# Smaller first loads in order of use, other buffers for GLA factors and gates, and new slot counts in a one-core hybrid decoder step

## The chip, the cores and the metric

One core of one Trainium2 chip runs the whole kernel. The metric is the device time of one execution in microseconds; three runs of the kernel before gave 998.02, 1000.86 and 1001.59 us, median 1000.86. One further execution was profiled: 999.49 us, of which 997.7 us lie between its first and its last instruction (the span).

## The reference, cut to what matters

One step of a two-layer recurrent trunk with 2048 features, over 256 prompt tokens and 8 x 8 sample tokens, 320 columns in all:

```
layer 0: proj = rmsnorm(x) @ w_in                     # q, k, v, gates, low-rank decay inputs
         q_a, k_a, v_a = silu(conv4(proj[qkv]))       # 8 heads x 128
         o_a, S_a = gated_delta_rule(q_a, k_a, v_a, g, beta, S_a)
         gk = log_sigmoid(proj[lr] @ w_lr + b) / 16   # "decays"
         o_b, S_b = gla(q_b, k_b, v_b, gk, S_b)       # 4 heads x (128, 256)
         x += concat(o_a, o_b) * silu(gate) @ w_out
layer 1: x += (rg_lru(conv4(rmsnorm(x) @ w_x)) * silu(rmsnorm(x) @ w_g)) @ w_out
out:     rmsnorm(x), and all recurrent and convolution states of prompt and samples
```

## The kernel before, in words

Features lie on the 128 partitions and the 320 token columns along the free axis. Every dense product is run as 30 groups of 512 output features. A group (`run_group`, L246) holds four PSUM accumulators of 128 x 320 and goes through 8 chunks `kc`; a chunk is 2 x 128 input features (index `a`) times 512 outputs, 512 KB of weights `wst`. `split_chunk` (L231) splits each half chunk into a rounded part `wh` (ScalarE) and a remainder `wl` (VectorE), `split_x` (L1403) does the same for the activations (`xh`, `xl`), and `product` (L255) issues three matmuls of 320 columns for each pair of 128 x 128 (wh xh, wh xl, wl xh; L261). A chunk is thus 24 matmuls and a group 192.

All other work lies between these matmuls. It is written as generators in three queues: `hi`, `lo` and `tails`. After each product pair half `slot` (L130) advances the front of each queue by one step, so a group gives 64 steps. The table `WAITS` says how many empty steps a generator leaves at each named place (`wait`, L66). `until(flag)` (L412) advances `lo` without matmuls between until a flag is set; `drain` empties a queue. The framework orders the instructions of each engine by this order and by its own estimates of readiness; each engine then runs its own list in order. SyncE (SP) issues nearly all loads.

The groups in order: 0 Q, 1 K, 2 V, 3 V second half, 4 K second half, 5 Q second half of the delta rule (`evac_conv_a`, L417); 6 to 9 the GLA's q, k, v, v (`evac_plain`); 10 to 13 the four gates (`evac_gate`, L1366); 14 to 17 the output product; 18 to 25 the LRU inputs and gates; 26 to 29 the last product. On the queue `lo` stand, one after another: `small_work`, `gla_decays` (L1174), `delta_half(0)`, `delta_half(1)`, `delta_sample` (L878), `gla` (L1321). Their places in this order, in steps after group 0 began: the first two start after group 1 (step 128), `gla` is appended after group 8. After group 13 all queues are drained. `sample_states(0, 16)` runs in groups 14 to 17 and `sample_states(16, 24)` (L982) in groups 26 to 29; the latter loads the samples' GLA states, updates and stores them.

`gla_decays` keeps its factors in two tiles that take both buffers of the tag VP, which the V halves of groups 2 and 3 need; so group 2 calls `until("gd")` in its last chunk. Gates 0 and 1 keep their sample columns in the tiles `SMPQ` and `SMPK` that `delta_sample` reads, so they call `until("gdns")` in the last chunk of group 10. At the end y is scaled in pieces (L1916 to L1919) and each piece is stored when it is ready.

Of the kernel before, what the change touches and what calls it, by code (L numbers as in the profile page):

```python
# [71 lines left out]
def hybrid_step(ctx, tc, x_cols, w_dense, w_small, w_lr, w_gate, par_a, par_b, par_c, gains, head_rows,  # L72
# [141 lines left out]
    def load_first():  # L214

        t = wst[0] = wpool.tile([P, 2, 512], F32, name="wst", tag="wst", bufs=3)
        for n in (0, 256):
            sp.dma_start(t[:, 0, n:n + 256], w_dense[0, 0, :, 0, n:n + 256])
        load_x(sp, 1, 1)
        sp.dma_start(t[:, 1], w_dense[0, 0, :, 1])  # L220
# [25 lines left out]
    def run_group(g, hook=None, n_lo=1):  # L246
# [3 lines left out]
        for kc in range(8):  # L250
# [18 lines left out]
            for f in range(4):  # L269
                if hook:  # L270
                    hook(kc, f)
                for a in range(2):
                    if i or a:
                        product(f, a)
                    if a == 0:
                        slot(n_lo)
# [140 lines left out]
    def evac_conv_a(slot_name, half, part):  # L417
# [8 lines left out]
        def late():  # L426
            if part == 2:
                until("gd")
            p_ = env["keep"] if part == 0 else env["lay0b"]
            st["t"] = p_.tile([P, 4, TP], F32, name="qkv", tag=("QP", "KP", "VP")[part], bufs=2)  # L430
            env[slot_name, half] = st["t"]
# [742 lines left out]
    def gla_decays():  # L1174
# [3 lines left out]
        r3 = [env["lay0b"].tile([P, 4, TP], dt, name="lr3", tag="VP", bufs=2).rearrange("p a b -> p (a b)")[:80]  # L1178
              for dt in (F32, F32R)]
# [186 lines left out]
    def evac_gate(idx, dst):  # L1366
        st = {}

        def late():
# [6 lines left out]
            until("gdns")  # L1376
            if idx == 3:
                until(("gp", 1))
            p_ = env["keep"] if tag == "QP" else env["lay0b"]
            st["z"] = (p_.tile([P, 4, TP], F32, name="zp", tag=tag, bufs=2), env["SMP" + tag[0]].rearrange("p u q e x -> p (u q e x)")[:, :4 * TS].rearrange(  # L1380
                             "p (f t) -> p f t", f=4))
# [318 lines left out]
    load_chunk(1)  # L1700
    load_x(sp, 2, 2)
    load_x(sp, 4, 2)
    load_chunk(2)
# [85 lines left out]
    with tc.issue_after(env["xs"][0].ins):  # L1789
        x_tile(1)  # L1790
        split_chunk(0, 1)
    with tc.issue_after(env["xs"][1].ins):
        for a in range(2):
            split_chunk(1, a)
    hi.append(start_work())

    def hook0(kc, f):
        if f == 0 and kc < 4:
            load_x(sp, 8 + 2 * kc, 2)
        if f % 2 and kc < 7:  # L1800
            k = 2 * (kc + 1) + f // 2
            x_tile(k)
# [19 lines left out]
    for nm in ("qs16", "kns", "krs"):  # L1822
        env[nm] = lay0b.tile([P, 4, TS], F32, name=nm)

# [91 lines left out]
    for m, f, n in ((0, 0, 1), (0, 1, 1), (0, 2, 2), (1, 0, 4), (2, 0, 4), (3, 2, 2)):  # L1916
        t = ob[m][:, f:f + n]
        dve.tensor_mul(t, t, row[:, None, :].to_broadcast([P, n, NT]))  # L1918
        sp.dma_start(y_cols[m, :, f:f + n], t)  # L1919
# [62 lines left out]
```

## Time and profile before

| what | value |
|---|---|
| three runs | 998.02, 1000.86, 1001.59 us |
| profiled execution, whole | 999.49 us |
| its span | 997.7 us |
| TensorE matmul busy | 971.5 us |
| VectorE, ScalarE, GpSimd busy | 708.4, 525.5, 229.9 us |
| mean granted TensorE clock | 0.992 |

TensorE is the engine that is nearly always busy. Where it stands, and where its clock is at the lower level, is read from its list of waits, from the timeline and from windows of time; the granted clock is 1.00 at 2.4 GHz and 0.50 at 1.2 GHz.

### The profile page before, as it was taken

Reading aid. Unit: us, or ns where it says so; the run is one execution under the profiler, and the core shown is the slowest. Engines: PE = TensorE matmul, PEld = TensorE weight load, DVE = VectorE, ACT = ScalarE, POOL = GpSimd, SP = SyncE. Lnnn points to the kernel's source line nnn. Section 1 sums busy time; section 2 is a strip of 40 time slices with the busy share of each in tenths; the row PEclk is TensorE's granted clock in tenths of the full one; section 3 lists DMA queues with packets and bytes.
Section 4 is the critical chain, followed back from the end, with each engine's and each line's share of the span. In section 5 each row is a group of like instructions: output and inputs, shape, how many; then the busy total and the mean of one; then the engine's idle time right before and its main releaser. Section 6 shows DMA issues by size and latency. Waiting matters only on the chain. (4 is left out here: it accounts for less than half of the span.)

```text
span 997.7 us, 18739 instructions
## 1 busy us (share of the span) xinstructions
PE 971.5 (97%) x6917; PEld 952.5 (95%) x6917; DVE 708.4 (71%) x1483; ACT 525.5 (53%) x1077; POOL 229.9 (23%) x365
## 2 busy tenths in 40 slices
PE   8999999999999999999999999999999999999995
PEld 8989999999999998899999999999999999999995
DVE  6789877675454556687677789867969668776753
ACT  7567674456333444665233344547685885333441
POOL 4520026702083020152112333200010000054000
PEclk8999999999999999999999999999999999999998
DMA  8535435534455266243766887654546435568742
GB/s 290 168 122 144 135 111 175 144 117 127 139 154 163 87 227 223 70 136 108 270 224 199 256 264 243 217 158 145 158 123 191 131 125 170 166 184 309 265 139 105
DMA packets 63927, 171.62 MB, mean 172 GB/s; under 512 B 16248, under 2 KB 21388, under 8 KB 63324
## 3 DMA queue, kind: packets, MB, share of 16 engines
q1 hardware_dynamic: 58852, 160.35, 51.3%
q0 software_dynamic: 2720, 8.66, 2.4%
q10 hardware_dynamic: 2264, 1.42, 0.4%
q8 instruction: 54, 0.88, 0.4%
q14 instruction: 37, 0.30, 0.1%
HBM read 155.73 MB, written 14.68 MB: 171 GB/s over the span
## 5 line engine op out<-in xcount | busy, mean ns | idle before, releaser
L261 PE MATMUL acc<-xh,wh 128*128 128x320 f32 x1920 | 600.6, 313 | 5.9 <-ACT wh L236 2.4
L261 PE MATMUL acc<-xh,wl 128*128 128x320 f32 x1920 | 595.3, 311 | 2.3 <-DVE wl L237 2.3
L261 PE MATMUL acc<-xl,wh 128*128 128x320 f32 x1920 | 596.8, 311 | 0.0
L236 ACT ACTIVATE wh<-wst 128x512 fp32r<-128x512 f32 x479 | 278.4, 623 | 326.7 <-PE acc L261 237.8
L237 DVE TENSOR_TENSOR wl<-wst,wh 128x512 fp32r<-128x512 f32 x479 | 337.2, 736 | 144.4 <-ACT wh L236 137.8
L261 PEld LDWEIGHTS acc<-xh,wh 128*128 128x128 f32 x1920 | 361.9, 189 | 9.4 <-ACT wh L236 5.4
L261 PEld LDWEIGHTS acc<-xh,wl 128*128 128x128 f32 x1920 | 362.0, 189 | 3.2 <-DVE wl L237 2.9
L261 PEld LDWEIGHTS acc<-xl,wh 128*128 128x128 f32 x1920 | 362.4, 189 | 1.3
L458 DVE SCALAR_TENSOR_TENSOR yc<-slab,pa,yc 128x344 f32<-128x344 f32 x72 | 42.2, 605 | 2.7 <-ACT yc L101 2.3
L1572 POOL MEMSET aa<- 128x32 f32 x4 | 0.7, 164 | 117.7 <-ACT rr L1559 66.7
L693 POOL TENSOR_TENSOR xi<-xi,tmp 128x60 f32<-128x60 f32 (+24 forms) x62 | 26.6, 429 | 4.9
L691 POOL TENSOR_TENSOR tmp<-ab,xi 128x60 f32<-128x60 f32 (+24 forms) x62 | 25.6, 412 | 4.8
L1002 POOL TENSOR_TENSOR uvkh<-uvk,uvkh 32x256 fp32r<-32x256 f32 (+1 forms) x8 | 12.3, 1542 | 56.8 <-DMA ugt<-in_state_gla_dram 51.4
L1007 POOL TENSOR_TENSOR uvm<-uvh,rm 96x512 fp32r<-96x512 f32 x16 | 20.5, 1307 | 0.3
L1114 POOL DMA_DIRECT2D out_s_delta_dram<-ust x8 | 6.0, 751 | 62.3 <-DVE ust L1111 62.3
L748 POOL TENSOR_TENSOR so<-so,mhalf 128x4 f32<-128x4 f32 x4 | 4.4, 1103 | 67.3 <-DVE so L747 67.3
L1111 DVE SCALAR_TENSOR_TENSOR ust<-ust,es,sn 128x128 f32<-128x128 f32 x64 | 17.8, 340 | 3.0 <-PE sn L1107 3.0
L462 ACT ACTIVATE qkv<-yc 128x256 f32<-128x256 f32 x24 | 10.0, 415 | 16.1 <-DVE yc L458 16.1
L1503 DVE SCALAR_TENSOR_TENSOR yc<-slab,pb,yc 128x344 f32<-128x344 f32 x32 | 17.6, 573 | 0.7 <-ACT yc L1501 0.6
L101 ACT ACTIVATE yc<-slab,pa 128x344 f32<-128x344 f32 x24 | 13.3, 576 | 8.6 <-DVE slab L350 7.0
L349 DVE TENSOR_TENSOR slab<-acc,rb 128x256 f32<-128x256 f32 x36 | 14.9, 417 | 2.6 <-PE acc L261 2.4
L376 POOL MEMSET slab<- 128x12 f32 x10 | 1.2, 124 | 65.5 <-DVE xc L1510 36.3
(464 smaller groups left out, 1019.0 us busy)
## 6 DMA issues: line engine op xcount, KB each, us to landing
wst<-in_w_dense_dram SPq DMA_DIRECT2D x239, 512.0 KB
st<-in_state_delta_dram SPq DMA_DIRECT2D x8, 512.0 KB
st<-in_state_gla_dram SPq DMA_DIRECT2D x4, 1024.0 KB
ust<-in_state_delta_dram SPq DMA_DIRECT2D x8, 512.0 KB
out_s_delta_dram<-ust POOLq DMA_DIRECT2D x8, 512.0 KB, 4.7
ugt<-in_state_gla_dram SPq DMA_DIRECT2D x8, 512.0 KB
out_s_gla_dram<-ugt POOLq DMA_DIRECT2D x8, 512.0 KB, 7.1
x0r<-in_x_cols_dram SPq DMA_DIRECT2D x8, 320.0 KB
```

The lines of the kernel that those rows point to most:

```text
L101: return act.activation(out, in_, AF.Identity, scale=scale)
L236: act.activation(h, wst[i][:, a, :], AF.Copy)
L237: env["last_split"] = dve.tensor_sub(l, wst[i][:, a, :], h.bitcast(F32))
L261: mm = pe.matmul(o, (h, h, l)[j][:, fs], (xh, xl, xh)[j][k], start=(k == 0 and j == 0), stop=(k == KT - 1 and j == 2))
L349: dve.tensor_mul(xp[:, 3:259], xp[:, 3:259] if acc is None else acc[:, :256], rb[:, :256])
L458: dve.scalar_tensor_tensor(y[:, :n], xp[:, j:j + n], pa[:, ft, j:j + 1], y[:, :n], op0=OP.mult, op1=OP.add)
L691: behind(pool.tensor_mul(tv, ab[:, j, j + 1:, None].to_broadcast([P, m, w]), xi[:, j:j + 1, :w].to_broadcast([P, m, w])))
L693: behind(pool.tensor_add(xi[:, j + 1:, :w], xi[:, j + 1:, :w], tv))
L1002: pool.tensor_sub(o, t[rows, :, cols], o.bitcast(F32))
L1007: pool.tensor_mul(m, src.bitcast(F32)[:, None, :].to_broadcast([R, 4, P]), rm4[:R, :, None].to_broadcast([R, 4, P]))
L1111: dve.scalar_tensor_tensor(s_, s_, es[:, col:col + 1], ps[:, b, :], op0=OP.mult, op1=OP.add)
L1503: dve.scalar_tensor_tensor(y[:, :n], xp[:, j:j + n], pb[:, ft, 2 + j:3 + j], y[:, :n], op0=OP.mult, op1=OP.add)
```

## The change

It does the following.

- Start: the first three weight chunks are loaded as half chunks and the activations x in single tiles, in the order x0, w0a (still in two quarters), x1, w0b, x2, w1a, x3, w1b, x4, w2a, x5, w2b (a and b are the halves `a` = 0 and 1). Activation tiles 1 to 3 and the half chunks up to w1b are split before the first group begins. In chunks 1 and 2 the products go through all four accumulators for `a` = 0 first, then for `a` = 1.
- The two tiles of the GLA factors move from the tag VP to one buffer of QP and one of KP. `until("gd")` moves from the V groups (2, 3) to the second halves of K and Q (groups 4, 5).
- Gates 0 and 1 get sample tiles of their own (`zs0`, `zs1`); only gate 3 still calls `until("gdns")`.
- The y stores of rows 1 and 2 are cut in two.
- Some 50 entries of `WAITS` change. Those that the prediction uses are in the table below; sums of steps are for the whole generator.

| generator | entries changed | steps before | after |
|---|---|---|---|
| small_work | .2 0 to 1, .3 0 to 6 | 3 | 10 |
| gla_decays | .1 13 to 16, .3 4 to 7, .4 9 to 10 | 70 | 86 |
| delta_half, each | quad_a.1 3 to 2, invert32.3 3 to 2, quad_out.3 3 to 0, quad_b.1 22 to 23, .2 1 to 4, .5 0 to 2, .9 2 to 1 | 218 | 214 |
| delta_sample | invert.2 6 to 2, .1 12 to 8, .4 9 to 8, .5 14 to 8, .7 11 to 10, .8 0 to 1, quad_a.1 | 159 | 112 |
| gla | gla.1 2 to 0, .2 4 to 5, .3 3 to 2, .4 19 to 20, gla_out.1 6 to 3, .2 2 to 3 | 214 | 196 |
| sample_states(16, 24), a pair of units | .8 12 to 2, .10 6 to 10 | 36 | 42 |

The diff without the table of waits:

```diff
     def load_first():
-        t = wst[0] = wpool.tile([P, 2, 512], F32, name="wst", tag="wst", bufs=3)
-        for n in (0, 256):
-            sp.dma_start(t[:, 0, n:n + 256], w_dense[0, 0, :, 0, n:n + 256])
-        load_x(sp, 1, 1)
-        sp.dma_start(t[:, 1], w_dense[0, 0, :, 1])
+        for i in range(3):
+            t = wst[i] = wpool.tile([P, 2, 512], F32, name="wst", tag="wst", bufs=3)
+            for a in range(2):
+                if i or a:
+                    load_x(sp, 2 * i + a, 1)
+                w = 512 if i or a else 256
+                for n in range(0, 512, w):
+                    sp.dma_start(t[:, a, n:n + w], w_dense[0, i, :, a, n:n + w])
...
-                    if i or a:
+                    if 0 < i < 3:
+                        product((2 * f + a) % 4, f // 2)
+                    elif i or a:
                         product(f, a)
...
         def late():
-            if part == 2:
+            if part < 2 and half:
                 until("gd")
...
-        r3 = [env["lay0b"].tile([P, 4, TP], dt, name="lr3", tag="VP", bufs=2).rearrange("p a b -> p (a b)")[:80]
-              for dt in (F32, F32R)]
+        r3 = [t.rearrange("p a b -> p (a b)")[:80] for t in env["lr3"]]
...
             tag = ("QP", "KP", "", "VP")[idx]
-            until("gdns")
             if idx == 3:
+                until("gdns")
                 until(("gp", 1))
...
-            st["z"] = (p_.tile([P, 4, TP], F32, name="zp", tag=tag, bufs=2), env["SMP" + tag[0]].rearrange("p u q e x -> p (u q e x)")[:, :4 * TS].rearrange(
-                             "p (f t) -> p f t", f=4))
+            zs = env["zs"][idx] if idx < 2 else env["SMPV"].rearrange("p u q e x -> p (u q e x)")[:, :4 * TS].rearrange(
+                "p (f t) -> p f t", f=4)
+            st["z"] = (p_.tile([P, 4, TP], F32, name="zp", tag=tag, bufs=2), zs)
...
     load_first()
-    load_chunk(1)
-    load_x(sp, 2, 2)
-    load_x(sp, 4, 2)
-    load_chunk(2)
     load_x(sp, 6, 2)
...
-    with tc.issue_after(env["xs"][0].ins):
-        x_tile(1)
-        split_chunk(0, 1)
-    with tc.issue_after(env["xs"][1].ins):
-        for a in range(2):
-            split_chunk(1, a)
+    for k in range(1, 4):
+        with tc.issue_after(env["xs"][k - 1].ins):
+            x_tile(k)
+            split_chunk(k // 2, k % 2)
...
-        if f % 2 and kc < 7:
+        if f % 2 and 0 < kc < 7:
...
+    env["lr3"] = [p_.tile([P, 4, TP], dt, name="lr3", tag=tag, bufs=2)
+                  for p_, tag, dt in ((ws0, "QP", F32), (lay0b, "KP", F32R))]
+    env["zs"] = [ws0.tile([P, 4, TS], F32, name=f"zs{i}") for i in range(2)]
...
-    for m, f, n in ((0, 0, 1), (0, 1, 1), (0, 2, 2), (1, 0, 4), (2, 0, 4), (3, 2, 2)):
+    for m, f, n in ((0, 0, 1), (0, 1, 1), (0, 2, 2), (1, 0, 2), (1, 2, 2), (2, 0, 2), (2, 2, 2), (3, 2, 2)):
```

## Rows read from the trace of the kernel before

**Rows 1.** The page: busy time and share of the span of each engine.

```profile
PE 971.5 (97%) x6917; PEld 952.5 (95%) x6917; DVE 708.4 (71%) x1483; ACT 525.5 (53%) x1077; POOL 229.9 (23%) x365
```

**Rows 2.** The chain of work that ended last, a stretch of it with nothing between the matmuls: start, duration, what and how many.

```profile
637.00 51.91 PE acc L261 x354
```

**Rows 3.** The list of waits for TensorE over the whole span: who waited for whom, us in total, times, longest.

```profile
PE ot L964 <- DVE on L959: 3.0, 2, 1.6
PE acc L261 <- ACT wh L236: 2.4, 2, 1.5
PE acc L261 <- DVE wl L237: 2.3, 2, 1.8
PE acc L261 <- ACT xh L101: 1.7, 1, 1.7
...
PE got L1168 <- DVE gon L1164: 1.2, 2, 0.6
PE acc L261 <- DVE slab L350: 1.2, 1, 1.2
...
PE smt L498 <- DVE sm L487: 0.9, 1, 0.9
...
PE cum L528 <- DVE gt L521: 0.4, 1, 0.4
```

**Rows 4.** Windows at the start: stretch and its length, busy us (and instructions) of PE, PEld, DVE, ACT and POOL, then granted clock, DMA share and GB/s.

```profile
0.00:7.00 7.00, 5.58 (x27) 4.96 (x27) 3.08 (x10) 3.66 (x6) 5.24 (x13) 1.00 0.67 192
7.00:8.00 1.00, 1.00 (x7) 1.00 (x8) 0.66 (x1) 0.00 (x0) 0.00 (x0) 1.00 0.88 305
8.00:9.00 1.00, 1.00 (x7) 0.75 (x6) 0.00 (x0) 0.00 (x0) 0.00 (x0) 1.00 1.02 399
9.00:10.75 1.75, 0.02 (x2) 0.01 (x1) 1.00 (x2) 1.66 (x4) 0.00 (x0) 1.00 1.01 405
...
10.75:12.40 1.65, 1.65 (x10) 1.65 (x10) 1.65 (x5) 0.85 (x2) 0.36 (x1) 0.73 1.01 410
...
12.40:18.20 5.80, 5.80 (x23) 5.80 (x23) 4.80 (x12) 5.55 (x13) 3.28 (x7) 0.50 0.80 278
```

**Rows 5.** The timeline at the start: start, duration, engine, line, operation, out<-in, count, and in brackets the idle time before and what ended it.

```profile
6.31 0.63 ACT L236 ACTIVATE wh<-wst 128x512 fp32r<-128x512 f32 x1 [0.59 <-DMA wst<-in_w_dense_dram]
6.97 0.69 DVE L237 TENSOR_TENSOR wl<-wst,wh 128x512 fp32r<-128x512 f32 x1 [0.67 <-ACT wh L236]
...
9.09 1.15 ACT L236 ACTIVATE wh<-wst 128x512 fp32r<-128x512 f32 x2 [2.15 <-DMA wst<-in_w_dense_dram]
...
10.14 1.46 ACT L101 ACTIVATE xh<-ob,gcol 128x320 fp32r<-128x320 f32 x3
10.74 0.58 PEld L261 LDWEIGHTS acc<-xh,wh 128*128 128x128 f32 x4 [1.99 <-ACT xh L101]
```

**Rows 6.** Windows around the end of group 2, the same columns as rows 4.

```profile
105.00:110.90 5.90, 5.90 (x41) 5.72 (x39) 5.59 (x14) 5.06 (x10) 0.00 (x0) 1.00 0.04 11
110.90:112.90 2.00, 0.17 (x3) 0.01 (x1) 2.00 (x5) 0.60 (x1) 0.00 (x0) 1.00 0.00 0
...
113.90:117.30 3.40, 3.40 (x15) 3.40 (x15) 3.40 (x8) 1.14 (x3) 0.00 (x0) 0.50 0.69 190
```

**Rows 7.** The timeline of VectorE there (L1207 is the scan of the decays), and TensorE's next matmul.

```profile
110.95 0.81 DVE L1207 TENSOR_TENSOR_SCAN gk<-seg,gk 128x320 f32<-128x320 f32 x1
...
112.89 0.57 PE L261 MATMUL acc<-xh,wl 128*128 128x320 f32 x2 [1.83 <-DVE wl L237]
```

**Rows 8.** The timeline of TensorE: the first instruction of `delta_half(0)`, `delta_half(1)` and `delta_sample`, and the output transposes of `delta_sample`.

```profile
122.75 0.60 PE L580 MATMUL kt<-ident,qkv 128*128 128x128 f32 x4
...
239.82 0.60 PE L580 MATMUL kt<-ident,qkv 128*128 128x128 f32 x4
...
357.24 0.60 PE L580 MATMUL kt<-ident,smpK 128*128 128x128 f32 x4
...
397.78 0.33 PE L964 MATMUL ot<-ident,on 128*128 128x128 f32 x1 [1.42 <-DVE on L959]
...
410.05 0.30 PE L964 MATMUL ot<-ident,on 128*128 128x128 f32 x1 [1.61 <-DVE on L959]
```

**Rows 9.** The timeline at the end of `gla`: the issues of its sample states on SP, its two state products, the first matmul of group 14, and the last transposes.

```profile
479.88 1.18 SPq L1332 DMA_DIRECT2D st<-in_state_gla_dram x2
...
491.17 1.93 PE L1357 MATMUL gpo<-st,gqm 128*32 128x256 f32 x32
...
493.13 0.81 SPq L1332 DMA_DIRECT2D st<-in_state_gla_dram  x2
...
503.23 1.93 PE L1357 MATMUL gpo<-st,gqm 128*32 128x256 f32 x32
...
505.44 0.49 PE L261 MATMUL acc<-xh,wh 128*128 128x320 f32 x1
...
507.86 0.44 PE L1168 MATMUL got<-ident,gon 128*128 128x128 f32 x2 [0.61 <-DVE gon L1164]
```

**Rows 10.** The chain of waits in groups 26 and 27.

```profile
913.92 9.73 DMA wst<-in_w_dense_dram
```

**Rows 11.** Windows at the end, the same columns as rows 4 (y is being stored).

```profile
989.00:990.00 1.00, 0.00 (x0) 0.00 (x0) 1.00 (x2) 0.00 (x0) 1.00 (x1) 1.00 0.88 311
990.00:991.00 1.00, 0.00 (x0) 0.00 (x0) 1.00 (x2) 0.00 (x0) 0.45 (x1) 1.00 0.85 329
991.00:992.00 1.00, 0.00 (x0) 0.00 (x0) 1.00 (x1) 0.00 (x0) 0.00 (x0) 0.57 0.72 279
```

40 rows, old and new, of the table WAITS are left out of this document.

## The prediction

> **What bounds the kernel now.** I read the page's busy times first: the matmul engine is busy 97% of the span, every other engine 71% or less [rows 1]. Then the chain of waits for a stretch without interruptions: 354 matmuls in 51.91 us, 146.6 ns each [rows 2]. The program has 30 x 192 = 5760 such matmuls, 845 us at that pace. The change touches no matmul's size or number, so all it can win is time in which TensorE stands, time in which its clock is low, and the tail after the last matmul. Third, therefore, TensorE's own list of waits [rows 3]: the rows shown add up to 13.1 us. Fourth, the windows around the two longest, for the granted clock: 0.50 (1.2 GHz) from 12.4 to 18.2 us, after TensorE stood from 9.0 to 10.75 [rows 4], and from 113.9 to 117.3, after it stood from 110.9 to 112.9 [rows 6]. Elsewhere I found no stretch at the low level before the last matmul. Each gap thus cost its own length and something after it.
>
> **The start.** Chunk 1 was one load of 512 KB; ScalarE waited for it until 9.09, split both halves (1.15 us for two) and only then turned to x2 at 10.14; TensorE went on at 10.74 after an idle of 1.7 us [rows 3, 5]. The new order asks for less before that point: x0, w0a, x1, w0b, x2, w1a are 3 x 164 KB + 3 x 262 KB = 1.28 MB (in thousands of bytes), where before x2 stood behind all of chunk 1. The old run moved 7.0 x 192 = 1.34 MB by 7.0 us [rows 4], so w1a should land near 6.8. ScalarE ends w0b's split at 6.94; then x2 (a third of 1.46 = 0.49 us) and w1a's split (0.58) take it to 8.0, and VectorE's remainder of 0.69 to 8.7 [rows 5]. TensorE is busy with chunk 0 until 9.0, so the gap closes with 0.3 us to spare. x3 and w1b (1.70 MB) come by 8.1 at the 305 to 399 GB/s of the next rows [rows 4]; their splits end near 9.9, and the four products of `a` = 0 (12 x 0.147 = 1.76 us) keep TensorE until 10.8. Behind the added issues on SP stand x6/x7 and chunk 3; chunk 3 waits for chunk 0's buffer in any case, so I cost them at nothing; without that cover it would be some 0.4 us an issue. Gain: 1.7 us of idle. The clock: 5.8 us at 0.50 and 1.65 us at 0.73 [rows 4] are worth 0.5 x 5.8 + 0.27 x 1.65 = 3.3 us; I take 3.1, since some tiny matmuls of the masks fall into it. Sum 4.8, with 0 and 5.1 as ends.
>
> What speaks against it is the speed of small loads. The Trainium skill, "DMA: Bandwidth & Descriptors", section "Rules for kernel authors", asks for 1 MiB and more in a DMA and for the merging of small ones. Rows 4 agree in kind: 305 GB/s at 7 to 8 us, with pieces still in the queues, against 399 to 405 when only large ones ran. By its row for 64 KB (138 GB/s) an estimate is 1.28 MB / 138 = 9.3 us, and the gap would stay.
>
> **The decays.** `until("gd")` in group 2's last chunk forced the rest of `gla_decays` into the same few microseconds as the group's evacuation. In steps: 128 + 3 + 70 = 201 was its natural end, and the call comes at 128 + 57 = 185. VectorE ran the scans (0.81 us each) ahead of the split that TensorE needed, and TensorE stood for 1.83 us [rows 7]; the DMA share fell to 0.04 and 0.00 because no weight buffer came free [rows 6]. After: 128 + 10 + 86 = 224, no V group calls, and the call in group 4 comes at 256 + 57 = 313, long after. `delta_half(0)` stands behind it on `lo`: it is appended only after group 2's conv tails (four of 9 empty steps), and its first transposes ran at 122.75 [rows 8], which I count as step 222; 2 steps later is nothing. Gain 1.8 idle and half of 3.4 us of clock = 1.7: 3.5, ends 1.0 and 4.0. The wait of `cum` (0.4) gets 6 steps of cover: 0.4 [rows 3].
>
> **The samples of the delta rule.** The three first transposes lie 117.1 and 117.4 us apart [rows 8], and the table of waits gives 218 steps for a `delta_half`: 0.54 us a step, so the count can be trusted. `delta_sample` had 159 steps, 86 us, yet its second output transposes ran at 410.05, only 53 us after its first instruction: `until("gdns")` squeezed it, and TensorE stood 1.42 and 1.61 us at these transposes. After, nothing squeezes it before group 13, and it has 112 steps, 10 of them between the scaling and the transposes. Gain 3.0, ends 1.5 and 3.0. Where this goes: it starts 6 steps earlier (8 fewer in the halves, 2 more before) and ends 112 x 0.54 - 3 = 57 us after 357.24, at about 414 on the old clock, 4 us later than before. `gla` follows with 196 steps, 106 us: 520, where it ended at 508 before [rows 9]. Group 14 began at 505.4 [rows 9]. It needs the last sample GLA outputs for its last quarter, 144 matmuls or 21 us in; 15 us late plus the gating and split of about 3 us still fits, with 3 us to spare. I cost it at 1 us, because TensorE already stood 0.6 us twice at `got` [rows 3] and the space there shrinks from 8 to 6 steps; ends 0 and 8.
>
> **Last group's states.** In groups 26 and 27 TensorE waited 2.4 us for `wh` [rows 3], behind a weight load that took 9.73 us [rows 10] while state loads and stores came in pairs. The units are now evenly spaced (22 and 20 steps instead of 24 and 12), but the first fetches keep their places. Half of it: 1.2, ends 0 and 2.4. `sample_states(0, 16)` and the LRU entries move work where TensorE hardly stands; cost 0.5, ends -0.5 and 2.
>
> **The tail.** From 989 to 992 the DMA share was 0.88, 0.85 and 0.72 [rows 11]; 0.55 us of transfer were missed while VectorE scaled whole rows. Halves start the stores earlier: 0.4, ends -0.2 and 0.55.
>
> **The sum** against the profiled execution of 999.49 us: 4.8 + 3.5 + 0.4 + 3.0 + 1.2 + 0.4 = 13.3 gained, 1.0 + 0.5 lost: 987.7, say 988. The median of the runs is 1.4 us above that execution; I make no correction for it. The waits of group 1's end (slab 1.2, `smt` 0.9) [rows 3] hang on the first row norm, whose chain has the same number of steps, and stay.
>
> **Rivals.** (a) The start gains little: w1a or ScalarE is late by more than 0.3 us and the clock still falls. At a mean of 192 GB/s [rows 4] x3 and w1b (1.70 MB) land at 8.9 and their splits end near 10.6, which still holds; at 20% less, 154, w1a lands at 8.3, its remainder is ready at 10.1 and the gap is 1.1 us. The start then gives 0.7 instead of 4.8: 992. The page on DMA named above would lead here. (b) The gaps at 1.42 and 1.61 us [rows 8] were not followed by a low clock, those of 1.7 and 1.83 were, so a gap's clock cost is not fixed; runs of before may not all have paid 4.6 us of clock. The Trainium skill, "TensorE: Matmul & The Clock Gate", section "What's actually happening", calls the observation window free-running, which would do this; rows 4 and 6 against rows 8 agree with it. It gives 988 for the new kernel all the same, but a run of it with one fall left is at 990. (c) GLA comes too late (slower). 960 - 896 = 64 of its steps are undone when the queues are drained. The first state load took 11.3 us from issue to product (479.88 to 491.17), the second, which goes out after the first product, 10.1 (493.13 to 503.23) [rows 9]. If both begin only after group 13 and the framework puts these products ahead of group 14's matmuls, TensorE, in order, stands up to 21 us, plus two falls of the clock at 1.7: 988 + 23 = 1011. It makes the kernel slower than before once more than about 13 us fall on TensorE. For it: the drain. Against it: the last state product at 503.23 already ran with at most 0.6 us of standing beside it. (d) The orders move and other gaps of the same kind open, since the framework makes a new order everywhere: 13 us gained, some 10 lost, 998.
>
> **How the numbers follow.** Forecast 988: 0.56 with (b) inside it; (a) 992: 0.20; a milder (c), 5 to 7 us at group 14, 994: 0.11; (d) 998: 0.08; (c) in full, 1011: 0.05. Low end: all upper ends, 999.5 - 5.1 - 4.0 - 0.4 - 3.0 - 2.4 - 0.55 - 0.5 = 983.5, less 0.5 for new slack: 983. High end 996 leaves (d) and (c) in full out. A measurement of this kernel tells 0.5% (5 us) from no change. Faster by over that (under 995.9): 0.87; within: 0.08; slower: 0.05.
>
> **What would show it.** Right: no idle of TensorE between 9 and 11 us and clock 1.00 in 12 to 18; at the end of group 2 no gap and a DMA share well above 0.04; no wait of `ot`; `gla`'s last transposes some 10 us into group 14 with no gap over 1 us there; no weight load of 9 us before group 27; a DMA share near 1 from 990 on in the tail. Wrong: a gap at group 14's third or last quarter, new waits of `got` or `y`, a low clock anywhere before the last matmul.

## The result and the profile after

The changed kernel took 993.66 us (median of 5 runs, 993.0 to 995.18) beside 999.76 (5 runs, 998.02 to 1001.59) of the kernel before: ratio 0.9945, interval 0.9929 to 0.9961. Run again later (experiment e9 below) it gave 995.08 (12 runs, 993.62 to 998.78) beside 997.58 (23 runs, 994.87 to 1000.06): 0.9986, interval 0.9971 to 1.0001. The intervals don't meet; most of the difference is in the kernel before, whose medians on the chips of the experiments were 996.05, 997.89, 997.58 and 997.63. The clock has a part in the rest: the granted clock of the changed kernel was 0.996 in the mean of its first five runs and 0.993 in the twelve of e9, beside 0.995 in the 23 runs of the kernel before there. By the two measurements the change is worth 0.6% and 0.1%; forecast was 1.2%.

The profiled execution of the changed kernel took 994.33 us, span 992.6, mean granted clock 0.995. Its page, engine by engine (answers to [rows 1]):

```profile
PE 969.5 (98%) x6917; PEld 950.5 (96%) x6917; DVE 707.5 (71%) x1485; ACT 532.9 (54%) x1083; POOL 220.2 (22%) x365
```

TensorE's list of waits in it (who waited for whom: us in total, times, longest; `...` stands for rows left out, here and below), the answer to [rows 3]:

```profile
PE got L1173 <- DVE gon L1169: 2.3, 4, 0.7
PE acc L264 <- DVE wl L240: 1.5, 2, 0.7
PE gsn L1126 <- POOL uvm L1012: 1.3, 1, 1.3
PE acc L264 <- DVE xl L1411: 1.3, 2, 0.8
...
PE acc L264 <- DVE slab L355: 1.2, 1, 1.2
PE acc L264 <- DVE xh L1410: 1.1, 2, 0.8
...
PE cum L533 <- DVE gt L526: 0.7, 1, 0.7
```

The waits for `ot` (3.0 us), for `wh` (2.4) and for the start's `xh` (1.7) are gone. New are `gsn` (1.3), `xl` and `xh` (2.4 together, in another place), 1.1 more at `got` and 0.3 more at `cum`; of `wl` 1.8 went with the decays and 0.7 came at 25 us. Windows of the same run (columns as in [rows 4]) answer to [rows 4, 6, 11]:

```profile
5.00:12.00 7.00, 6.76 (x40) 6.42 (x41) 5.42 (x12) 4.72 (x11) 1.76 (x3) 1.00 0.97 317
12.00:18.00 6.00, 6.00 (x43) 6.00 (x42) 5.21 (x11) 5.93 (x13) 1.40 (x7) 1.00 1.01 393
...
92.00:95.50 3.50, 3.50 (x15) 3.50 (x14) 2.81 (x6) 0.06 (x1) 0.00 (x0) 0.52 0.57 163
...
108.00:115.00 7.00, 7.00 (x50) 7.00 (x49) 7.00 (x14) 5.35 (x13) 0.00 (x0) 1.00 0.51 158
...
984.00:987.00 3.00, 0.00 (x0) 0.00 (x0) 3.00 (x5) 0.00 (x0) 1.33 (x1) 0.87 0.95 356
```

Both old low-clock stretches are gone (1.00 at 12 to 18, no gap from 108 to 115 and a DMA share of 0.51 instead of 0.00 to 0.04), but a new one lies at 92 to 95.5, behind the wait for `cum`. Besides the end, the clock was low for 10.2 us in the first profile of the kernel before and for 3.4 us in this one. At half the clock that is 5.1 against 1.7 us, so an estimate of 3.4 of the 5.1 us between the two spans is clock.

How far the changed run is ahead is read from the timeline: group n begins with the (192 n + 1)th matmul of the dense line (L261 before, L264 after). After less before, in us: group 1 -3.4, group 5 -5.7, group 11 -5.3, group 16 -4.3, group 26 -4.1, group 29 -5.4, last dense matmul -5.1, end of the span -5.1. So 1.0 us of the lead is lost between 378 and 560 us, where the 3.0 us of `ot` should have been added to it. (Between these two groups the lead can't be read in this way: group 14 begins 18.8 us earlier, because GLA work that stood before it now stands behind its start.) The loss lies in the gating and split of the last GLA outputs. There the timeline of VectorE and GpSimd reads (start, duration, engine, line, operation; in brackets the idle time before and what ended it):

```profile
519.06 0.88 DVE L1411 TENSOR_TENSOR xl<-ob,xh 128x320 fp32r<-128x320 f32 x2
...
520.51 0.42 DVE L1003 CAST ukh<-uk 96x512 fp32r<-96x512 f32 x1
522.77 0.42 DVE L1003 CAST uvh<-uv 96x512 fp32r<-96x512 f32 x1 [1.84 <-DMA uv<-wv_scratch]
523.11 0.32 DVE L1410 CAST xh<-ob 128x320 fp32r<-128x320 f32 x1
...
524.35 1.39 DVE L1410 CAST xh<-ob 128x320 fp32r<-128x320 f32 x1
525.77 1.24 DVE L1411 TENSOR_TENSOR xl<-ob,xh 128x320 fp32r<-128x320 f32 x1
526.94 2.97 DVE L240 TENSOR_TENSOR wl<-wst,wh 128x512 fp32r<-128x512 f32 x2
...
523.33 2.23 POOL L1007 TENSOR_TENSOR uvh<-uv,uvh 32x512 fp32r<-32x512 f32 x1 [0.97 <-PE acc L264]
525.63 5.17 POOL L1012 TENSOR_TENSOR uvm<-uvh,rm 96x512 fp32r<-96x512 f32 x4
```

Two things are to be seen. VectorE, which runs its list in order, stood 1.84 us for a sample transfer (`uv`) although the last two x splits behind it are what TensorE needs. And once that transfer had released GpSimd's work on it, the last split ran beside GpSimd: 1.39 us instead of 0.32 for a cast, 1.24 instead of 0.44 (half of 0.88) for a remainder. TensorE stood 2.4 us for `xh` and `xl` there.

### The profile page after: what moved, and what is told of

Read it like the earlier page. It is cut to its first block, busy times and chain, and to the rows that moved or that the text cites. A ratio compares the mean times of both kernels' runs of the same rounds, so it can differ in the third digit from the quotient of the medians.

```text
span 992.6 us, 18768 instructions
## 1 busy us (share of the span) xinstructions
PE 969.5 (98%) x6917; PEld 950.5 (96%) x6917; DVE 707.5 (71%) x1485; ACT 532.9 (54%) x1083; POOL 220.2 (22%) x365
## 4 chain that ended last, share of the span: by engine, by line
PE 44%; DVE 2%; DMA 2%; POOL 1%; issue 1%; SPq 0%; DVEq 0%; ACT 0%; POOLq 0%
PE acc L264 42%; DMA uv<-wv_scratch 1%; DMA ugt<-in_state_gla_dram 1%; POOL uvkh L1007 1%; DVE wl L240 1%; DVE ob L1921 0%; PE lg L1549 0%; PE lg L1550 0%; PE lg L1548 0%; PE gsn L1126 0%; PE sn L1112 0%; DVE xh L1410 0%; PE fsp L1670 0%; POOL gso L1166 0%; SPq L996 0%
## 5 line engine op out<-in xcount | busy, mean ns | idle before, releaser
L264 PE MATMUL acc<-xh,wh 128*128 128x320 f32 x1920 | 601.2, 313 | 2.7 <-DVE slab L355 1.2
L264 PE MATMUL acc<-xl,wh 128*128 128x320 f32 x1920 | 595.1, 310 | 1.3 <-DVE xl L1411 1.3
L264 PE MATMUL acc<-xh,wl 128*128 128x320 f32 x1920 | 594.5, 310 | 1.7 <-DVE wl L240 1.5
L240 DVE TENSOR_TENSOR wl<-wst,wh 128x512 fp32r<-128x512 f32 x479 | 332.3, 726 | 146.2 <-ACT wh L239 143.8
L264 PEld LDWEIGHTS acc<-xh,wh 128*128 128x128 f32 x1920 | 361.6, 188 | 6.0 <-issue 1.9
L264 PEld LDWEIGHTS acc<-xl,wh 128*128 128x128 f32 x1920 | 361.6, 188 | 3.4 <-DVE xl L1411 1.8
L264 PEld LDWEIGHTS acc<-xh,wl 128*128 128x128 f32 x1920 | 360.8, 188 | 3.5 <-DVE wl L240 2.8
L1130 DVE SCALAR_TENSOR_TENSOR ugt<-ugt,ebs,gsn 128x256 f32<-128x256 f32 x32 | 14.1, 472 | 4.3 <-PE gsn L1126 4.3
```

Source lines behind the costliest of these rows:

```text
L240: env["last_split"] = dve.tensor_sub(l, wst[i][:, a, :], h.bitcast(F32))
L264: mm = pe.matmul(o, (h, h, l)[j][:, fs], (xh, xl, xh)[j][k], start=(k == 0 and j == 0), stop=(k == KT - 1 and j == 2))
L1130: dve.scalar_tensor_tensor(s_, s_, ebs[:, h, 4 * hb + b + i:4 * hb + b + i + 1], ps[:, i * 256:(i + 1) * 256], op0=OP.mult, op1=OP.add)
```

## The experiments

Ratios are to the kernel before on the same chip, with 95% intervals. Entries of `WAITS` in the diffs are cut out of longer lines of the table. e1 to e4, e5 to e8, e9 to e12, and e13 with e14 shared a chip each.

**e1, the casts later.** The slot ahead of the first two casts:

```diff
-    "sample_states.11": 5,
+    "sample_states.11": 35,
```

> The changed kernel with the empty steps between the first state load and the first cast of sample_states(0, 16) raised from 5 to 35; nothing else. Theory A (VectorE's casts of the state rows stand ahead of the last two activation splits of group 14, wait there for a load that lands late, and GpSimd's masked copies then slow those splits): the standing of TensorE on xh and xl at 523 to 528 us (2.4 us) falls under 0.5, the waits on got stay near 2.3, and the kernel gains 2 to 3 us on the changed one, about 991. Rival B (the late GLA outputs alone delay the splits): the standing stays at 2 us or more, 994. Rival C: the states, started later, run into the next norm, and 1 to 3 us come back after group 17: 993 to 995 without the standing at 523.

Measured: 1003.35 us, ratio 1.0067 (1.0045 to 1.0088). On the spot the standing is gone (group 16 starts 9.8 us earlier than in the kernel before, against 4.3), but the list of waits of its trace names what came for it:

```profile
PE sn L1112 <- POOL uvm L1012: 3.6, 2, 3.2
PE acc L264 <- DVE ob L1453: 2.8, 1, 2.8
...
PE gsn L1126 <- POOL uvm L1012: 2.1, 1, 2.1
```

All 16 units slid 30 steps towards the norm behind group 17, and the gaps there were followed by 13.7 us at the low clock, as the window shows:

```profile
618.80:632.50 13.70, 10.02 (x33) 8.37 (x33) 12.55 (x32) 3.15 (x6) 10.43 (x11) 0.50 0.76 253
```

The cause was confirmed at its place, the mend was none; the price of sliding was far above what was expected. e11 tries it without the slide.

**e2, the gates back home.** The changed kernel, gates 0 and 1 as before:

```diff
+            until("gdns")
             if idx == 3:
-                until("gdns")
...
-            zs = env["zs"][idx] if idx < 2 else env["SMPV"].rearrange("p u q e x -> p (u q e x)")[:, :4 * TS].rearrange(
...
-            st["z"] = (p_.tile([P, 4, TP], F32, name="zp", tag=tag, bufs=2), zs)
+            st["z"] = (p_.tile([P, 4, TP], F32, name="zp", tag=tag, bufs=2), env["SMP" + tag[0]].rearrange("p u q e x -> p (u q e x)")[:, :4 * TS].rearrange(
...
```

> The changed kernel with the sample columns of gates 0 and 1 back in the tiles that delta_sample reads, and with the forced run of delta_sample in group 10's last chunk back; all else as changed. Theory A: the two standings on ot come back (3.0 us), GLA ends before or at the start of group 14 again, and the 4.6 us lost between group 11 and group 16 vanish but for the old 0.6 on got: in sum 0.5 to 2 us faster than the changed kernel, 992 to 993. Rival B (the loss at group 14 comes from the new step counts of GLA and of the states, not from the move): it stays, and the 3.0 us come on top: 997.

Measured: 993.0 us, ratio 0.9955 (0.9933 to 0.9977), as good as the full change. No standing at `got`, `xh` or `xl`, and in their place a wait of 1.4 us for `ot` and one of 1.8 for `y`.

**e3, the start alone**, on the kernel before:

```diff
+        for i in range(3):
+            t = wst[i] = wpool.tile([P, 2, 512], F32, name="wst", tag="wst", bufs=3)
+            for a in range(2):
+                if i or a:
+                    load_x(sp, 2 * i + a, 1)
...
-                    if i or a:
+                    if 0 < i < 3:
+                        product((2 * f + a) % 4, f // 2)
...
```

> The kernel before with the start alone changed: finer loads in order of use, early splits, order of the products in chunks 1 and 2. Theory: no idle at 9 to 10.7 us and no low clock at 12 to 18; group 1 begins 3.4 us earlier (as in the changed kernel), with the wait on wl at 25 us that is new there; all later gaps as before: 996 to 997. Forecast of the prediction for this term: 4.8 us, 995. Rival: the finer loads do not decide, and the gap stays, 999 to 1000.

Measured: 996.77 us, ratio 1.0004 (0.9989 to 1.0019): the start by itself gained at most 1.1 us, against 4.8 in the forecast's sum. Its profile is the first sign that gaps and clock are not tied. The windows show the old gap of 1.8 us before the end of group 2, and the clock stays up behind it (compare [rows 6]):

```profile
108.00:111.00 3.00, 1.17 (x8) 0.90 (x8) 3.00 (x6) 1.28 (x1) 0.00 (x0) 1.00 0.00 0
111.00:115.00 4.00, 4.00 (x29) 4.00 (x28) 4.00 (x9) 1.53 (x4) 0.00 (x0) 1.00 0.66 175
```

**e4, the decays alone**, on the kernel before:

```diff
-            if part == 2:
+            if part < 2 and half:
                 until("gd")
...
+    env["lr3"] = [p_.tile([P, 4, TP], dt, name="lr3", tag=tag, bufs=2)
+                  for p_, tag, dt in ((ws0, "QP", F32), (lay0b, "KP", F32R))]
```

> The kernel before with the two factor tiles in QP and KP and the forced end of the decays moved to groups 4 and 5; old step counts. Theory: the gap of 2 us at 110.9 and the low clock behind it vanish, 3.5 us: 996 to 997. Rival: another gap of the same kind opens where the decays now run, and 1 us or less is gained, 999.

Measured: 993.98 us, ratio 0.9979 (0.9961 to 0.9997). The gap at 110 is down to 0.4 us. The old start stands here for 1.3 us before 8.5, and no low clock follows it, where [rows 4] had one.

**e5, the kernel before once more**, with no edit.

> The kernel before, unchanged, profiled a second time. It asks whether the low-clock stretches that the sum credited to the change belong to the kernel or to one execution. Theory A (a fall of the granted clock does not belong to its gap): the standing of TensorE is at the same places as in the first profile (1.7 us at 9 to 10.7, about 2.1 us near 110, 1.7 and 1.6 us before the ot transposes at 397 and 410, the xh waits at 887 and 918), but at least one of the two low-clock stretches (11.5 to 18.35 and 113.9 to 117.3) is missing or lies elsewhere; the ratio is 1.00 within 0.3%, and single runs spread over 4 to 7 us. Theory B (gap and fall go together): both stretches come back within 1 us of their places in this execution too.

Measured: 997.62 us, ratio 0.9991 (0.9976 to 1.0007), single runs 995.16 to 1002.21. The profiled execution (1002.21) has its gaps at the same instructions; the windows (with their granted clock, the third number from the end) show

```profile
12.90:16.40 3.50, 3.50 (x15) 3.50 (x15) 3.05 (x8) 3.50 (x8) 3.02 (x7) 0.51 0.90 312
...
112.00:115.30 3.30, 3.30 (x15) 3.30 (x13) 3.30 (x7) 1.09 (x3) 0.00 (x0) 0.50 0.63 179
...
924.30:931.10 6.80, 6.10 (x23) 6.13 (x24) 5.75 (x13) 3.34 (x6) 0.60 (x1) 0.50 0.46 141
```

The fall at the start is half as long as in [rows 4], that of group 2 is there, and a third stands at 924, where the first profile had none. That is neither theory as it was put: both falls came back, the first of them shorter, and a fall more came behind a wait that had been there without one (in e5 it is longer, up to 2.7 us for `wh`).

**e6, the slots alone.** The kernel before with the new `WAITS`, 41 entries in all.

```diff
-    "delta_sample.1": 12, "gla.4": 19, "sample_states.11": 11, "sample_states.8": 12,
+    "delta_sample.1": 8, "gla.4": 20, "sample_states.11": 5, "sample_states.8": 2,
...
```

> The kernel before with the new slots alone; the start, the decays' homes and the gates' homes stay as they were. Theory A (the move of the gates, not the slots, pushed the GLA work late): no standing of TensorE over 1 us on xh or xl at 523 to 531, and group 16 starts no later than in the kernel before, at most 0.5 us; the waits for dense weights at 887 and 918 go (about 3 us), the wait for cum near 90 grows by 0.3 to 0.7, so 1 to 3 us faster than before at equal clock, ratio about 0.998. Rival (the slots did it, above all the cast slot cut from 11 to 5): 3 to 5 us of standing at 523 to 531 here too, and the ratio is 1.000 to 1.003.

Measured: 999.28 us, ratio 1.0013 (0.9993 to 1.0032); no standing at 523 to 531, so the slots by themselves don't make it. But the expected gain didn't come either. The list of waits of its trace:

```profile
PE ot L964 <- DVE on L959: 3.1, 2, 1.8
...
PE y L933 <- DMA XT<-xt_scratch: 1.8, 1, 1.8
PE gsn L1121 <- POOL uvm L1007: 1.5, 1, 1.5
```

The `ot` waits are whole, and a wait of `y` for its transposed input is new. Shorter slots in `delta_sample` are of no use while `until("gdns")` squeezes it all the same.

**e7, the gates alone**, on the kernel before: only the tiles `zs0` and `zs1`.

```diff
-            until("gdns")
             if idx == 3:
+                until("gdns")
...
+    env["zs"] = [ws0.tile([P, 4, TS], F32, name=f"zs{i}") for i in range(2)]
```

> The kernel before with the gates' sample factors for the first two gates in tiles of their own, so that these two gates no longer wait for the delta rule's samples; nothing else. Theory A: the groups of products 12 and 13 come earlier and the GLA work later than in the kernel before, so that TensorE stands 3 to 5 us more between 480 and 531 than before's got waits did; the ot waits at 397 and 410 (3.0 us) may go with it; in all +0 to +3 us, ratio 1.000 to 1.003. Rival (slots did it): no more standing at 480 to 531 than in the kernel before, the ot waits go or shrink, ratio 0.997.

Measured: 1011.58 us, ratio 1.0139 (1.0113 to 1.0166): a miss, far beyond the 3 us expected. No `ot` wait is left, and the list of waits of its trace, cut to 495 to 560 us, reads

```profile
PE acc L261 <- DVE xh L1406: 4.6, 2, 3.3
PE got L1168 <- DVE gon L1164: 3.0, 3, 2.1
PE gpo L1357 <- DMA st<-in_state_gla_dram: 3.0, 2, 2.4
```

with 13.6 us at the low clock between 509 and 543. The state loads for `gpo` were issued from 500.8 on; in the changed kernel, with its slots, from 486.8.

**e8, the old slots.** The changed kernel with the old `WAITS` (e6's diff the other way).

> The changed kernel with the slots of the kernel before; start, decays and gates as in the change. Theory A: the loss ahead of group 16 stays (3 to 5 us of standing between 480 and 531), the waits at 887 and 918 come back (about 3 us), the ot waits stay gone if they belong to the gates: 1 to 4 us slower than the changed kernel, ratio to the kernel before 0.997 to 0.999. Rival (the slots pushed the GLA work late): the loss ahead of group 16 is under 1 us, ratio 0.992 to 0.995 in spite of the waits at the end.

Measured: 1009.19 us, ratio 1.0122 (1.0096 to 1.0149): again a miss in size, with e7's three waits within 0.1 us. So the gates' move costs some 14 us by itself, and the new slots take most of that back; alone they gain nothing.

**e9, the changed kernel once more**, with no edit.

> The changed kernel, unchanged, profiled a second time on the chip of the three others, so that they can be compared with it. Theory A: the standing of TensorE is where it was (cum near 89, got waits, xh and xl at 523 to 530, gsn near 877), ratio 0.993 to 0.997; whether the clock falls after the wait for cum (91.9 to 95.3 in the first profile) may differ. Theory B (a fall belongs to its gap): the same stretch is low again.

Measured: 995.08 us, ratio 0.9986 (0.9971 to 1.0001). The gaps are the same ones, and the clock falls elsewhere, as the windows of its trace show:

```profile
86.00:92.00 6.00, 5.31 (x37) 4.49 (x35) 5.37 (x18) 2.99 (x6) 0.74 (x2) 1.00 0.53 173
92.00:96.00 4.00, 4.00 (x30) 4.00 (x29) 3.74 (x8) 1.39 (x3) 0.00 (x0) 1.00 0.47 154
...
526.50:533.50 7.00, 6.26 (x24) 6.26 (x25) 5.36 (x7) 0.00 (x0) 4.48 (x4) 0.51 0.49 159
```

Behind `cum` the clock stayed up; behind the standing at 523 to 527, which cost no clock in the first profile, it was down for 6.8 us. The new start stood in this run, too, 1.3 us for the second half of the first weight chunk (its split began at 7.61, at 5.76 in the first profile).

**e10, start and decays together**, gates and slots as before (and the finer y stores): e3's and e4's edits in one.

> The changed start and the changed decays together (and the finer last stores of y), with the gates' homes and the slots of the kernel before. Theory A: these two carry the whole gain, and the gates' homes with the new slots come out at nothing: group 5 starts 5 to 6 us earlier than in the first profile of the kernel before, the ot waits at 390 to 405 (3.0 us) and the waits at the end (3 us) are there, nothing stands at 523 to 531, and the ratio is 0.994 to 0.997, as that of the full change. Rival (the gates' homes and the slots gain as forecast, 3.0 + 1.2 less 1.5): this kernel is 2 to 4 us slower than the full change on the same chip, ratio 0.998 to 1.000.

Measured: 994.7 us, ratio 0.9977 (0.9964 to 0.9991): not behind the full change (995.08) on the same chip, although `ot` and the weights are waited for as before, by the list of waits of its trace:

```profile
PE acc L264 <- DVE wl L240: 2.8, 4, 1.5
PE ot L969 <- DVE on L964: 2.7, 2, 1.4
PE acc L264 <- ACT wh L239: 1.3, 1, 1.3
```

**e11, the casts behind the splits.** The changed kernel; the delta half gets slots 15 to 17 of its own in place of 3 to 5, so that the units keep their places:

```diff
-    "sample_states.11": 5, "sample_states.2": 7, "sample_states.6": 6,
+    "sample_states.11": 34, "sample_states.2": 2, "sample_states.6": 4,
...
+    "sample_states.15": 2, "sample_states.16": 1, "sample_states.17": 3,
...
-        yield from wait("sample_states.3")
+        yield from wait("sample_states.15" if delta else "sample_states.3")
...
```

> The changed kernel with VectorE's first casts of uk and uv behind the last x splits of group 15 (slot 11 from 5 to 34), and the slots after them shortened for the delta half alone (2, 3, 4, 5 from 7, 14, 2, 8 to 2, 2, 1, 3, and 6 from 6 to 4), so that the later states keep their places; it mends what the first experiment broke. Theory A (the place in VectorE's list and the masks beside the splits cost the 3 to 4 us at 523 to 531): the standing there is under 1 us, group 16 starts 2.5 to 4 us earlier relative to group 14 than in the changed kernel, no pile-up before the norm, ratio 0.989 to 0.993. Rival (the time is given back): TensorE waits for the masks (uvm) before the first sn instead, 2 to 4 us, ratio as the changed kernel's.

Measured: 989.77 us, ratio 0.9934 (0.9917 to 0.9951), 5.3 us under the changed kernel on that chip. The same stretch in its timeline:

```profile
521.24 0.55 DVE L1410 CAST xh<-ob 128x320 fp32r<-128x320 f32 x2
521.71 0.49 DVE L1411 TENSOR_TENSOR xl<-ob,xh 128x320 fp32r<-128x320 f32 x1
...
522.72 0.48 DVE L1411 TENSOR_TENSOR xl<-ob,xh 128x320 fp32r<-128x320 f32 x1
523.12 0.42 DVE L1003 CAST ukh<-uk 96x512 fp32r<-96x512 f32 x1
523.64 0.42 DVE L1003 CAST uvh<-uv 96x512 fp32r<-96x512 f32 x1
524.15 3.31 DVE L240 TENSOR_TENSOR wl<-wst,wh 128x512 fp32r<-128x512 f32 x2
...
526.99 5.26 POOL L1012 TENSOR_TENSOR uvm<-uvh,rm 96x512 fp32r<-96x512 f32 x4
```

The splits run at full pace and are done at 523.2; `uv` is no longer waited for; only `wl`, which has time to spare, is still slow (3.31 us for two) beside GpSimd. One edit moved both the casts and GpSimd's work behind them, so it doesn't tell the share of the 1.84 us wait from that of the slow split. Group 16 starts 2.4 us further ahead of the kernel before than in the changed kernel's first profile (6.7 against 4.3), and 5.0 further than in e9, whose clock fell there.

**e12, gates back and the last states between old and new.** e2, and

```diff
-    "sample_states.8": 2, "sample_states.10": 10,
+    "sample_states.8": 8, "sample_states.10": 8,
```

> The second experiment (the changed kernel with the first two gates at home again) with the slots of the last states between the old and the new: 8 from 2 to 8 and 10 from 10 to 8. Theory A: the wait for gsn near 877 (1.9 us) goes or shrinks to under 0.5, the waits for dense weights at 887 and 918 stay under 1 us: 1 to 2 us faster than the second experiment, ratio 0.990 to 0.995. Rival: the waits for dense weights come back (1 to 3 us), ratio 0.995 to 0.998.

Measured: 990.73 us, ratio 0.9936 (0.9919 to 0.9953). The list of waits of its trace, cut to 870 to 925 us, has one row left, and it is neither `gsn` nor a weight:

```profile
PE acc L264 <- DVE ob L1634: 0.6, 1, 0.6
```

**e13, both mends.** e11's and e12's slots on the changed kernel, gates in their new tiles.

> The casts behind the splits (as in the experiment before last) and the middle slots of the last states (8 and 10 both 8) together, on the changed kernel with the gates' sample factors in their new tiles. If the two losses are separate (theory A): the wait for gsn near 877 (1.3 to 1.9 us) shrinks to under 0.5, all else as with the casts alone, so 1 to 1.5 us faster than that, about 988.5, ratio 0.991 to 0.994. If they share a cause (rival): the waits for dense weights at 885 and 918 take its place, no gain.

Measured: 988.97 us (988.15 to 990.97), ratio 0.9921 (0.9898 to 0.9943), the lowest median of all. The wait for `gsn`, 1.2 us in e11, is gone, and none for weights came in its place, so the two losses are separate by the list of waits; the 0.8 us below e11 is inside both intervals. From group 24 on nothing stands, as the window from 800 to 973 us shows (TensorE is busy for all of it):

```profile
800.00:973.00 173.00, 173.00 (x1185) 172.66 (x1183) 114.70 (x213) 79.91 (x133) 29.03 (x26) 1.00 0.58 187
```

**e14, the slots of cum.** e12 with

```diff
-    "small_work.2": 1, "small_work.3": 6,
+    "small_work.2": 0, "small_work.3": 0,
```

> The best kernel so far (first two gates at home again, 8 and 10 both 8) with the two slots ahead of the product cum back at 0 (small_work 2 and 3 from 1 and 6). Theory A (the new slots put VectorE's gt behind more of its work, and made the wait for cum longer, 0.7 against 0.4 us, the opposite of the forecast): the wait falls back to 0.3 to 0.5 us, 0 to 0.5 us faster than without this edit, and where the clock falls after that wait in one run in some, 1.7 us more. Rival (the slots are right and the wait is of another making): the wait grows or stays at 0.7.

Measured: 994.5 us, ratio 0.9974 (0.9956 to 0.9992), a miss for the whole: slower than e12. The wait for `cum` did fall to 0.3 us, as expected, but the queue `lo` now runs 7 steps earlier from there on, and its list of waits shows what it met:

```profile
PE ot L969 <- DVE on L964: 3.1, 2, 1.8
PE y L938 <- DMA XT<-xt_scratch: 1.8, 1, 1.8
...
PE nbt L664 <- ACT dtm L628: 1.2, 1, 1.2
```

The first two are the waits of e6, whose gates are at home as well. Beside e12, which had 1.4 us of `ot` and 1.7 of `y`, the 1.7 us more at `ot` and the 1.2 at `nbt` (at 129 us) are what came.

## Why the prediction was wrong, by its own steps

**The clock (3.1 at the start, 1.7 in the decays): mis-sized.** The sum was made against one execution of 999.49 us, whose clock was low for 10.2 us besides the end, and of the 5.1 us that this cost 4.8 were booked as the kernel's. They are not in every run. In the profiles here the standing of 1.8 us near 110 was followed by a fall in two of four (the first profile and e5, not e3 and e7); the start's standing of 1.1 us or more in two of five (the first profile and e5, not e4, e7 and e9); the wait for `cum`, at 0.7, in three of eight (the changed kernel's first profile, e2 and e11, not e1, e6, e9, e12 and e13). That is 7 of 17. The 84 later runs of the kernel before agree: their mean granted clock is 0.9947 where the profiled execution had 0.992, and 0.0027 of 998 us is an estimate of 2.7 us less lost to the clock. So the 4.8 us were worth about half of that over many runs, and the new kernel pays its own falls, 1.7 us in its first profile and 3.4 in e9. Rival (b) had named this. It was right that the 988 for the new kernel does not hang on what the kernel before paid, but the gain does: the base is itself some 2 us lower than in the first five runs. The Trainium skill, "TensorE: Matmul & The Clock Gate", section "What's actually happening", calls the observation window free-running; e9, the same gaps with the fall elsewhere, agrees with it.

**The start's idle (1.7): the gap went, most of the time did not.** Group 1 began at 35.8 to 36.6 us in the eleven profiles with the new start, and at 36.6, 36.6 and 37.8 in the three with the old start whose clock did not fall there (e6, e7, e4): about 0.5 us, by their medians. The lead of 3.4 us there in the first profiles is for the most part the fall, 6.8 us at half the clock. TensorE now stands 0.7 us for `wl` near 25.5 in all eleven, and some 0.6 us or more for `wh` between 6.5 and 9.8 in six of them. What the sum had wrong is when the loads land: it kept w0b's old time and had w1a land near 6.8. In five of the six TensorE waited for w0b (1.3 us in e9, where it came 1.9 us late), in e14 for w1a, and in the first profile, where w0b came in time, ScalarE waited 1.18 us for x2 and split it from 7.58 on, not 6.94. The rate of the small loads was not the trouble that the prediction feared: 317 GB/s from 5 to 12 us, far above the 138 of its estimate, though the kernel before moved 356 there.

**The decays (1.8 of idle): right.** The gap is gone or under 0.5 us in the profile of every kernel with the new homes, and e4 gained 2.1 us by its ratio. **cum (0.4 gained): wrong in sign.** With six steps of cover the wait was 0.7 us; e14 shows 0.3 without them. Steps were taken for time that TensorE gains, but what came last was `gt`, a chain of some twenty short operations on VectorE among the weight splits.

**ot (3.0): right**, also in its reason, the squeeze by `until("gdns")`: e7 has no such wait with the gates' move alone, e6 all of it with the slots alone.

**GLA late (1.0 lost): the step that failed.** Two sentences of it: "15 us late plus the gating and split of about 3 us still fits", and, of the sample states, "move work where TensorE hardly stands; cost 0.5". The 15 us held the start of group 14 at its old 505.4. With work moved out of groups 10 to 13 that start came earlier, and the last transposes came 30 us into the group, not 15:

```profile
486.65 0.50 PE L264 MATMUL acc<-xh,wh 128*128 128x320 f32 x1
...
517.00 0.44 PE L1173 MATMUL got<-ident,gon 128*128 128x128 f32 x2 [0.61 <-DVE gon L1169]
```

The sentence also forgot that VectorE's list is in order. With the GLA outputs late, the casts of `uk` and `uv` came to stand ahead of the last splits. Their slot had been cut from 11 to 5 in the change, but that was not it: in e7 and e8, with 11, they stand ahead too, and in e6, with 5, nothing stands. In e11 the last transposes come as late (517.8) and TensorE stands neither for `xh` nor for `xl`, so it is the casts and the work behind them that cost the time, not the lateness alone. Beside 1.1 us more at `got`, this cost 2.4 us of standing and up to 3.4 of clock (half of 6.8, e9), and e11 gave back 5.3 of it in the medians. The sum's 3.0 for `ot` and the loss here cancel: start and decays alone (e10) are as fast as the full change. Rival (c) in full, 1011 us, has the time of the gates' move without the slots (e7 1011.6, e8 1009.2), but by luck: it had TensorE stand up to 21 us for the states, and e7 has 3.0 us of that, 4.6 for `xh`, 3.0 at `got` and 13.6 us of low clock.

**Last states (1.2): right in size, by another sum.** The waits for `wh` went (2.4 in [rows 3]) and `gsn` came, with 1.3 us, because the masks on GpSimd now have 10 steps less before the first product that needs them; the lead grew by 1.3 from group 26 to 29. **The tail (0.4): not there.** The last dense matmul lies 14.8 us before the end in both profiles; the DMA share rose (0.95 from 984 to 987), the end did not move. **Other (0.5 lost): about right**, 0.3 behind group 17 in the first profile and 1.0 in e9.

Together, by the experiments: start, decays and y stores were forecast at 8.7 us and gave 2.3 by e10's ratio; gates and slots were forecast at 3.1 more and gave nothing beside e10 on the same chip (995.08 us in e9 against 994.7).

What stays open: why the start's loads land later in some runs, as the weight chunk of e9 did, and which part of the difference between 0.9945 and 0.9986 belongs to chips and which to where the clock happened to fall.

## What to carry to other kernels

Profile the kernel before more than once before a low-clock stretch is booked as a gain: the gaps return at the same instructions, the falls behind them not always. Where late work is moved later still, read the in-order list of each helper engine around its new place, not only the engine that bounds: one cast that waits for a transfer holds up every split behind it. And slots in a single queue are not local: seven steps at 90 us cost some 4 us from 129 us on (e14 against e12, by their ratios), so undo such a table entry by entry, with the places that follow held fixed, as e11 did after e1 had not.

## What the runs showed of the hardware

A fall of the clock did not depend on the length of the gap alone: 1.8 us of standing was followed by none in e3, 0.7 us by one of 3.4 us in three runs.

Some of VectorE's operations took two and a half to four times as long while GpSimd's elementwise work ran: a cast 1.39 us against 0.32, a remainder 1.24 against 0.48, two weight remainders 3.31 against 1.28. Not all did: in the first profile of the changed kernel a weight remainder (from 523.35) and an x remainder (from 523.95) kept their 0.68 and 0.48 us beside GpSimd's first operation, which itself took 2.23 us, against 1.29 for the same operation in the kernel before. The Trainium skill, "SBUF — State Buffer", section "SBUF: two separate sides", speaks of a pair of ports that these two engines share and that one holds for a whole instruction; the longer times on both engines agree with that, though no run here took GpSimd's work away to prove it. In e11 the same GpSimd work beside weight remainders, which have time to spare, cost nothing that shows.
